# Two neighbouring rows to a partition, skipping by 256-row halves, a staggered loop and one DMA queue in a masked softmax after a matrix product

## The chip, the cores and the metric

The kernel runs on one core of one Trainium2 chip. The metric is the device time of one execution in microseconds (us). Each kernel was run several times, and the median of its fast runs is quoted.

## The reference, cut to what matters

```python
batch, m, k, n = 16, 512, 512, 512          # x: (16, 512, 512) float32, weight: (512, 512) float32
mask = (np.triu(np.ones((m, n))) == 0)      # true strictly below the diagonal

y = scale * np.matmul(x, weight)
y = np.where(mask == 1, y, -1e9)
y_exp = np.exp(y - np.max(y, axis=-1, keepdims=True))
out = (y_exp / np.sum(y_exp, axis=-1, keepdims=True)).astype(np.float32)
```

Row r of an output keeps only the columns below r, so about half of the products can be skipped. Row 0 keeps none and becomes the constant 1/512. Every execution must read 16.78 MB of x and write 16.78 MB of output.

## The kernel before

One batch passes through these steps. GpSimd (POOL) issues a load that converts float32 to bfloat16 on its way into one of 16 buffers. TensorE (PE) transposes x in sixteen 128x128 blocks, and VectorE (DVE) and ScalarE (ACT) copy one half each of the transposed x out of PSUM. PE makes the products. ACT takes the exponential and its row sums. DVE takes the reciprocal of the sums and scales the rows. SyncE (SP) issues the store.

```python
X_BUFS = 16
OUT_BUFS = 6
x_r = x.rearrange("b (mt p) k -> b p mt k", p=P)          # 2 KB runs: one row each
out_r = out.rearrange("b (mt p) n -> b p mt n", p=P)

def load(b):
    xb = x_pool.tile([P, MT, K], BF16, name="xb")
    nc.gpsimd.dma_start(xb, x_r[b])
# ... prepare(b): sixteen transposes, then one copy on DVE and one on ACT ...
def multiply(b):
    for mt in range(MT):
        NC = (mt + 1) * P                                  # 128, 256, 384, 512 columns
        # ... four matmuls of NC columns, one mask product, one exponential with row sums ...
def normalise(b):
    nc.vector.reciprocal(rinv, st_sum.pop(b))
    # ... four scalings on DVE ...
def store(b):
    nc.sync.dma_start(out_r[b], ots[b % OUT_BUFS])
# ...
for b in range(B):
    if b + 1 < B:
        prepare(b + 1)
    multiply(b)
    normalise(b)
    store(b)
    if b + X_BUFS < B:
        load(b + X_BUFS)
```

The softmax here doesn't subtract the row's maximum and nothing guards it: scores larger than these inputs give would overflow.

Of the kernel before, what the change touches and what calls it, by code (L numbers as in the profile page):

```python
# [1 line left out]

# [5 lines left out]

FP32 = mybir.dt.float32
BF16 = mybir.dt.bfloat16  # L10
AF = mybir.ActivationFunctionType
ALU = mybir.AluOpType

MASK_NEG = -512.0
P = 128
X_BUFS = 16
OUT_BUFS = 6


@with_exitstack  # L20
def kernel(
    ctx: ExitStack,
    tc: tile.TileContext,
    x: bass.AP,
    weight: bass.AP,
    scale: float,
    mask: bass.AP,
    out: bass.AP,
):






    nc = tc.nc

    B, M, K = x.shape
    K2, N = weight.shape
    assert K == K2 and N == 512 and K == 512 and M == 512  # L40
    MT = M // P
    KT = K // P

    const = ctx.enter_context(tc.tile_pool(name="const", bufs=1))
    x_pool = ctx.enter_context(tc.tile_pool(name="xf", bufs=X_BUFS))
    xt_pool = ctx.enter_context(tc.tile_pool(name="xt", bufs=2))
    sum_pool = ctx.enter_context(tc.tile_pool(name="sums", bufs=4))
    psum_t = ctx.enter_context(tc.tile_pool(name="psum_t", bufs=4, space=bass.MemoryType.PSUM))
    psum_y = ctx.enter_context(tc.tile_pool(name="psum_y", bufs=4, space=bass.MemoryType.PSUM))

    x_r = x.rearrange("b (mt p) k -> b p mt k", p=P)
    out_r = out.rearrange("b (mt p) n -> b p mt n", p=P)

    ident_bf = const.tile([P, P], BF16, name="ident_bf")
    w_f32 = const.tile([P, KT, N], FP32, name="w_f32")
    w_bf = const.tile([P, KT, N], BF16, name="w_bf")
    diag_f32 = const.tile([P, MT, P], FP32, name="diag_f32")
    diag_bf = const.tile([P, MT, P], BF16, name="diag_bf")
    ots = [const.tile([P, MT, N], FP32, name=f"ot{i}") for i in range(OUT_BUFS)]

    st_x, st_xt, st_py, st_sum = {}, {}, {}, {}

    def load(b):
        xb = x_pool.tile([P, MT, K], BF16, name="xb")
        nc.gpsimd.dma_start(xb, x_r[b])  # L65
        st_x[b] = xb

    def prepare(b):

        xb = st_x.pop(b)  # L70
        xt = xt_pool.tile([P, KT, M], BF16, name="xt")
        for h in range(2):
            pt = psum_t.tile([P, 2, M], BF16, name="pt")
            for kk in range(2):
                kt = 2 * h + kk
                for mt in range(MT):
                    nc.tensor.transpose(  # L77
                        pt[:, kk, mt * P : (mt + 1) * P],
                        xb[:, mt, kt * P : (kt + 1) * P],
                        ident_bf,  # L80
                    )
            if h == 0:
                nc.vector.tensor_copy(xt[:, 0:2], pt)  # L83
            else:
                nc.scalar.copy(xt[:, 2:4], pt)  # L85
        st_xt[b] = xt

    def multiply(b):
        xt = st_xt.pop(b)
        ot = ots[b % OUT_BUFS]  # L90
        rsum = sum_pool.tile([P, MT], FP32, name="rsum")
        for mt in range(MT):
            NC = (mt + 1) * P
            py = psum_y.tile([P, N], FP32, name="py")
            for kt in range(KT):
                nc.tensor.matmul(  # L96
                    py[:, :NC],
                    lhsT=xt[:, kt, mt * P : NC],
                    rhs=w_bf[:, kt, :NC],
                    start=(kt == 0),  # L100
                    stop=(kt == KT - 1),
                )
            nc.tensor.matmul(  # L103
                py[:, mt * P : NC],
                lhsT=ident_bf,
                rhs=diag_bf[:, mt],
                start=False,
                stop=True,
                skip_group_check=True,
            )  # L110
            nc.scalar.activation(  # L111
                out=ot[:, mt, :NC],
                in_=py[:, :NC],
                func=AF.Exp,
                bias=0.0,
                scale=float(scale),
                accum_out=rsum[:, mt : mt + 1],
            )
        st_sum[b] = rsum

    def normalise(b):
        ot = ots[b % OUT_BUFS]
        rinv = sum_pool.tile([P, MT], FP32, name="rinv")
        nc.vector.reciprocal(rinv, st_sum.pop(b))  # L124
        for mt in range(MT):
            NC = (mt + 1) * P
            nc.vector.tensor_scalar_mul(ot[:, mt, :NC], ot[:, mt, :NC], rinv[:, mt : mt + 1])  # L127
        nc.gpsimd.memset(ot[0:1, 0, :P], 1.0 / N)  # L128

    def store(b):  # L130
        nc.sync.dma_start(out_r[b], ots[b % OUT_BUFS])  # L131

    make_identity(nc, ident_bf)


    load(0)
    nc.sync.dma_start(w_f32, weight.rearrange("(kt p) n -> p kt n", p=P))
    for mt in range(MT):
        nc.sync.dma_start(diag_f32[:, mt], mask[mt * P : (mt + 1) * P, mt * P : (mt + 1) * P])
    for b in range(1, X_BUFS):  # L140
        load(b)

    for ot in ots:
        for mt in range(MT - 1):
            nc.gpsimd.memset(ot[:, mt, (mt + 1) * P :], 0.0)  # L145
        nc.gpsimd.memset(ot[0:1, 0, P:], 1.0 / N)  # L146

    prepare(0)
    for kt in range(KT):
        if kt % 2 == 0:  # L150
            nc.vector.tensor_copy(w_bf[:, kt], w_f32[:, kt])  # L151
        else:
            nc.scalar.copy(w_bf[:, kt], w_f32[:, kt])  # L153
    nc.vector.tensor_scalar(  # L154
        out=diag_bf,
        in0=diag_f32,
        scalar1=-MASK_NEG,
        scalar2=MASK_NEG,
        op0=ALU.mult,
        op1=ALU.add,  # L160
    )

    for b in range(B):
        if b + 1 < B:
            prepare(b + 1)
        multiply(b)
        normalise(b)
        store(b)
        if b + X_BUFS < B:
            load(b + X_BUFS)  # L170


# [1 line left out]
_INS = ['x', 'weight', 'scale', 'mask']  # L174
_OUTS = [((16, 512, 512), 'float32')]

_NUMBERS = {'scale': 0.125}


# [26 lines left out]
```

## Time and profile before

| | before |
|---|---|
| median time | 94.33 us (94.16 to 94.41, four runs) |
| span of the profiled execution | 92.4 us |
| busiest compute engine | PE, 62% of the span |
| DMA row of the slices | 9 (90% or more) in 37 of 40 slices |

The span is what the profiler sees of one execution. The device time stands some 2 us above it. The prediction shows the main lines of the page. Beside the engines named above, PEld stands for PE's loading of its stationary operand and SPq for the transfers that SP issues; "clock" (PEclk) is the share of PE's full clock that was granted.

DVE in the steady part, in the timeline (start, duration, engine, line, operation, tiles, and in brackets the idle time before it with its releaser):

```profile
64.89 0.69 DVE L83 COPY xt<-pt 128x1024 bf16<-128x1024 bf16 x1 [0.86 <-PE pt L77]
65.50 0.17 DVE L124 RECIPROCAL rinv<-rsum 128x4 f32<-128x4 f32 x1
65.76 1.29 DVE L127 TENSOR_SCALAR ot<-ot,rinv 128x128 f32<-128x128 f32 x4
```

### The profile page before, as it was taken

To read this page: it belongs to the slowest core of one execution; us is meant where nothing else is said; L and a number is where in the kernel's file an instruction comes from. 1 tells how busy PE (TensorE), PEld (TensorE's weight loads), DVE (VectorE), ACT (ScalarE), POOL (GpSimd) and SP (SyncE) were. 2 spreads that over 40 slices of the span, in tenths; PEclk is the share of its full clock that TensorE was granted. 3 is DMA by queue.
4 is the path that set the end of the run, shared out by engine and by line. 5 is a ranking of instruction groups with operands and counts; after the bars stand their busy time and mean duration, and the time that the engine had idled before them with its cause. 6 is when DMAs were issued, how large, how long until landed. Compare 5 with 4: busy or idle time off the path is not lost.

```text
span 92.4 us, 1586 instructions
## 1 busy us (share of the span) xinstructions
PE 57.5 (62%) x568; PEld 43.1 (47%) x576; DVE 37.2 (40%) x99; ACT 47.0 (51%) x147; POOL 25.3 (27%) x62
## 2 busy tenths in 40 slices
PE   0000599999999999900019774699999999600000
PEld 0000568867876876900016352576786786200000
DVE  0030212458546799300004217276845853650000
ACT  5040044998789873400034091899878878700000
POOL 5993333222333999800001001011101110110000
PEclk9999999999999999996555699999999999995555
DMA  1899999999999999999999999999999999999990
GB/s 27 335 220 191 208 206 206 206 206 207 206 206 207 208 208 206 206 206 283 290 286 291 285 337 403 397 407 403 408 406 407 401 407 407 409 408 410 408 353 33
DMA packets 18007, 26.57 MB, mean 288 GB/s; under 512 B 592, under 2 KB 9296, under 8 KB 18000
## 3 DMA queue, kind: packets, MB, share of 16 engines
q0 software_dynamic: 8448, 8.39, 54.7%
q1 hardware_dynamic: 9552, 18.09, 52.5%
q8 instruction: 4, 0.07, 0.3%
q14 instruction: 3, 0.02, 0.1%
HBM read 18.09 MB, written 16.78 MB: 377 GB/s over the span
## 4 chain that ended last, share of the span: by engine, by line
DMA 44%; PE 23%; POOL 17%; DVE 1%; issue 1%; ACT 1%; DVEq 0%; SPq 0%; ACTq 0%; POOLq 0%
DMA xb<-in_x_dram 24%; DMA out_dram<-ot 20%; PE py L96 17%; POOL xb L65 7%; POOL ot L145 7%; PE pt L77 5%; POOL ot L146 2%; PE py L103 2%; DVE ot L127 1%; ACT ot L111 1%; POOL ot L128 1%; POOL ident_bf masks.py:199 0%; DVEq L201 0%; SPq L131 0%; POOL ident_bf masks.py:197 0%
## 5 line engine op out<-in xcount | busy, mean ns | idle before, releaser
L96 PE MATMUL py<-w_bf,xt 128*128 128x128 bf16 (+3 forms) x248 | 42.6, 310 | 12.2 <-ACT ot L111 11.6
L111 ACT ACTIVATE ot<-py 128x128 f32<-128x128 f32 (+1 forms) x64 | 27.5, 443 | 18.2 <-DMA out_dram<-ot 14.9
L96 PEld LDWEIGHTS <-xt 128*128 128x128 bf16 x256 | 22.2, 102 | 21.5 <-issue 13.4
L77 PE MATMUL pt<-ident_bf,xb 128*128 128x128 bf16 x256 | 18.1, 230 | 10.2 <-DMA xb<-in_x_dram 10.2
L127 DVE TENSOR_SCALAR ot<-ot,rinv 128x128 f32<-128x128 f32 (+1 forms) x64 | 23.2, 445 | 1.6 <-DVE rinv L124 0.5
L85 ACT COPY xt<-pt 128x1024 bf16<-128x1024 bf16 x16 | 16.2, 1016 | 10.8 <-PE pt L77 8.5
L77 PEld LDWEIGHTS <-xb 128*128 128x128 bf16 x256 | 16.3, 104 | 11.6 <-DMA xb<-in_x_dram 10.2
L83 DVE COPY xt<-pt 128x1024 bf16<-128x1024 bf16 x16 | 11.0, 689 | 15.9 <-PE pt L77 14.2
L65 POOL DMA_DIRECT2D xb<-in_x_dram x16 | 12.2, 770 | 16.4 <-DMA xb<-in_x_dram 16.1
L128 POOL MEMSET ot<- 1x128 f32 x16 | 4.3, 287 | 39.4 <-DVE ot L127 39.4
L103 PE MATMUL py<-diag_bf,ident_bf 128*128 128x128 bf16 x64 | 14.4, 225 | 0.0
L111 ACT ACTIVATION_READ_ACCUMULATOR ot<-py 128x1 f32 x64 | 13.4, 210 | 0.0
L124 DVE RECIPROCAL rinv<-rsum 128x4 f32<-128x4 f32 x16 | 2.7, 172 | 18.1 <-ACT ot L111 18.1
L103 PEld LDWEIGHTS <-ident_bf 128*128 128x128 bf16 x64 | 6.5, 102 | 3.4 <-issue 0.5
L145 POOL MEMSET ot<- 128x384 f32 (+2 forms) x18 | 6.3, 383 | 0.0
L151 DVE CAST w_bf<-w_f 128x512 bf16<-128x512 f32 x2 | 0.9, 481 | 5.9 <-DMA w_f<-in_weight_dram 5.9
L153 ACT CAST w_bf<-w_f 128x512 bf16<-128x512 f32 x2 | 1.1, 616 | 3.9 <-DMA w_f<-in_weight_dram 3.9
L146 POOL MEMSET ot<- 1x384 f32 x6 | 2.4, 408 | 0.0
L154 DVE TENSOR_SCALAR diag_bf<-diag_f 128x512 bf16<-128x512 f32 x1 | 0.4, 427 | 3.6 <-DMA diag_f<-in_mask_dram 3.6
L153 ACT ACT_TABLE_LOAD x1 | 1.3, 1283 | 0.7 <-PEq L187 0.7
masks.py:199 POOL TENSOR_SCALAR_AFFINE_SELECT ident_bf<-ident_bf 128x128 bf16<-128x128 bf16 x1 | 0.3, 307 | 0.1
masks.py:197 POOL MEMSET ident_bf<- 128x128 bf16 x1 | 0.2, 206 | 0.3 <-POOLq L187 0.3
(4 smaller groups left out, 0.4 us busy)
## 6 DMA issues: line engine op xcount, KB each, us to landing
out_dram<-ot SPq DMA_DIRECT2D x16, 1024.0 KB, 11.6
xb<-in_x_dram POOLq DMA_DIRECT2D x16, 512.0 KB, 21.0
w_f<-in_weight_dram SPq DMA_DIRECT2D x1, 1024.0 KB, 5.1
diag_f<-in_mask_dram SPq DMA_DIRECT2D x4, 64.0 KB, 6.5
```

The costliest lines, as they stand in the source:

```text
L65: nc.gpsimd.dma_start(xb, x_r[b])
L77: nc.tensor.transpose(pt[:, kk, mt * P : (mt + 1) * P], xb[:, mt, kt * P : (kt + 1) * P], ident_bf,)
L83: nc.vector.tensor_copy(xt[:, 0:2], pt)
L85: nc.scalar.copy(xt[:, 2:4], pt)
L96: nc.tensor.matmul(py[:, :NC], lhsT=xt[:, kt, mt * P : NC], rhs=w_bf[:, kt, :NC], start=(kt == 0), stop=(kt == KT - 1),)
L103: nc.tensor.matmul(py[:, mt * P : NC], lhsT=ident_bf, rhs=diag_bf[:, mt], start=False, stop=True, skip_group_check=True,)
L111: nc.scalar.activation(out=ot[:, mt, :NC], in_=py[:, :NC], func=AF.Exp, bias=0.0, scale=float(scale), accum_out=rsum[:, mt : mt + 1],)
L124: nc.vector.reciprocal(rinv, st_sum.pop(b))
L127: nc.vector.tensor_scalar_mul(ot[:, mt, :NC], ot[:, mt, :NC], rinv[:, mt : mt + 1])
L128: nc.gpsimd.memset(ot[0:1, 0, :P], 1.0 / N)
L145: nc.gpsimd.memset(ot[:, mt, (mt + 1) * P :], 0.0)
L146: nc.gpsimd.memset(ot[0:1, 0, P:], 1.0 / N)
```

## The change

The intent: partition p holds rows 2p and 2p+1 of a 256-row half, so that each partition moves runs of 4 KB in place of 2 KB. All transfers go through SP's one hardware queue, so no POOL load stands before the fills of the output buffers. The loads now bring float32, so DVE converts. The loop is written staggered: the cast of batch i+2, the transposes of i+1, the products of i, then scaling and store of i-1. With pairs of rows in a partition, skipping goes by halves, with 256 and 512 columns in place of 128, 256, 384 and 512.

```diff
-X_BUFS = 16
+X_BUFS = 6
-    x_r = x.rearrange("b (mt p) k -> b p mt k", p=P)
-    out_r = out.rearrange("b (mt p) n -> b p mt n", p=P)
+    x_r = x.rearrange("b (h p s) k -> b p h (s k)", h=2, s=2)
+    out_r = out.rearrange("b (h p s) n -> b p h (s n)", h=2, s=2)
     def load(b):
-        xb = x_pool.tile([P, MT, K], BF16, name="xb")
-        nc.gpsimd.dma_start(xb, x_r[b])
+        xf = x_pool.tile([P, QT, K], FP32, name="xf")
+        nc.sync.dma_start(xf.rearrange("p (h s) k -> p h (s k)", h=2), x_r[b])
+    def cast(b):
+        xb = xb_pool.tile([P, QT, K], BF16, name="xb")
+        nc.vector.tensor_copy(xb, st_x.pop(b))
     ... multiply(b):
-            NC = (mt + 1) * P
+            h = q // 2
+            NC = (h + 1) * HB                 # HB = 256
     ... mask tiles, fills of the output buffers and start: cut ...
-    for b in range(B):
-        if b + 1 < B:
-            prepare(b + 1)
-        multiply(b)
-        normalise(b)
-        store(b)
-        if b + X_BUFS < B:
-            load(b + X_BUFS)
+    for i in range(B + 1):
+        if i + 2 < B:
+            cast(i + 2)
+        if i + 1 < B:
+            transpose(i + 1)
+        if i < B:
+            multiply(i)
+        if i >= 1:
+            normalise(i - 1)
+            store(i - 1)
+            if i - 1 + X_BUFS < B:
+                load(i - 1 + X_BUFS)
```

More of the change, by code (lines that the diff above doesn't have):

```diff
@@ L40 @@
     assert K == K2 and N == 512 and K == 512 and M == 512
-    MT = M // P
+    QT = M // P
     KT = K // P
+    HP = P // 2
+    HB = 2 * P
     const = ctx.enter_context(tc.tile_pool(name="const", bufs=1))
     x_pool = ctx.enter_context(tc.tile_pool(name="xf", bufs=X_BUFS))
-    xt_pool = ctx.enter_context(tc.tile_pool(name="xt", bufs=2))
+    xb_pool = ctx.enter_context(tc.tile_pool(name="xb", bufs=3))
+    xt_pool = ctx.enter_context(tc.tile_pool(name="xt", bufs=3))
     sum_pool = ctx.enter_context(tc.tile_pool(name="sums", bufs=4))
@@ L56, with transpose @@
     w_bf = const.tile([P, KT, N], BF16, name="w_bf")
-    diag_f32 = const.tile([P, MT, P], FP32, name="diag_f32")
-    diag_bf = const.tile([P, MT, P], BF16, name="diag_bf")
-    ots = [const.tile([P, MT, N], FP32, name=f"ot{i}") for i in range(OUT_BUFS)]
-    st_x, st_xt, st_py, st_sum = {}, {}, {}, {}
+    diag_f32 = const.tile([P, QT, P], FP32, name="diag_f32")
+    diag_bf = const.tile([P, QT, HB], BF16, name="diag_bf")
+    ots = [const.tile([P, QT, N], FP32, name=f"ot{i}") for i in range(OUT_BUFS)]
+    st_x, st_xb, st_xt, st_sum = {}, {}, {}, {}
     def load(b):
-        xb = x_pool.tile([P, MT, K], BF16, name="xb")
-        nc.gpsimd.dma_start(xb, x_r[b])
-        st_x[b] = xb
-    def prepare(b):
-        xb = st_x.pop(b)
-        xt = xt_pool.tile([P, KT, M], BF16, name="xt")
-        for h in range(2):
-            pt = psum_t.tile([P, 2, M], BF16, name="pt")
-            for kk in range(2):
-                kt = 2 * h + kk
-                for mt in range(MT):
-                    nc.tensor.transpose(
-                        pt[:, kk, mt * P : (mt + 1) * P],
-                        xb[:, mt, kt * P : (kt + 1) * P],
-                        ident_bf,
-                    )
-            if h == 0:
+        xf = x_pool.tile([P, QT, K], FP32, name="xf")
+        nc.sync.dma_start(xf.rearrange("p (h s) k -> p h (s k)", h=2), x_r[b])
+        st_x[b] = xf
+    def cast(b):
+        xb = xb_pool.tile([P, QT, K], BF16, name="xb")
+        nc.vector.tensor_copy(xb, st_x.pop(b))
+        st_xb[b] = xb
+    def transpose(b):
+        xb = st_xb.pop(b)
+        xt = xt_pool.tile([P, KT, QT, P], BF16, name="xt")
+        for half in range(2):
+            pt = psum_t.tile([P, 2, QT, P], BF16, name="pt")
+            for kk in range(2):
+                kt = 2 * half + kk
+                for q in range(QT):
+                    nc.tensor.transpose(pt[:, kk, q], xb[:, q, kt * P : (kt + 1) * P], ident_bf)
+            if half == 0:
                 nc.vector.tensor_copy(xt[:, 0:2], pt)
@@ L90, in multiply @@
         ot = ots[b % OUT_BUFS]
-        rsum = sum_pool.tile([P, MT], FP32, name="rsum")
-        for mt in range(MT):
-            NC = (mt + 1) * P
+        rsum = sum_pool.tile([P, QT], FP32, name="rsum")
+        for q in range(QT):
+            h = q // 2
+            NC = (h + 1) * HB
             py = psum_y.tile([P, N], FP32, name="py")
@@ L97, in multiply @@
                     py[:, :NC],
-                    lhsT=xt[:, kt, mt * P : NC],
+                    lhsT=xt[:, kt, q],
                     rhs=w_bf[:, kt, :NC],
@@ L103, in multiply @@
             nc.tensor.matmul(
-                py[:, mt * P : NC],
+                py[:, h * HB : NC],
                 lhsT=ident_bf,
-                rhs=diag_bf[:, mt],
+                rhs=diag_bf[:, q],
                 start=False,
@@ L111, in multiply @@
             nc.scalar.activation(
-                out=ot[:, mt, :NC],
+                out=ot[:, q, :NC],
                 in_=py[:, :NC],
@@ L116, in multiply @@
                 scale=float(scale),
-                accum_out=rsum[:, mt : mt + 1],
+                accum_out=rsum[:, q : q + 1],
             )
@@ L122, in normalise @@
         ot = ots[b % OUT_BUFS]
-        rinv = sum_pool.tile([P, MT], FP32, name="rinv")
+        rinv = sum_pool.tile([P, QT], FP32, name="rinv")
         nc.vector.reciprocal(rinv, st_sum.pop(b))
-        for mt in range(MT):
-            NC = (mt + 1) * P
-            nc.vector.tensor_scalar_mul(ot[:, mt, :NC], ot[:, mt, :NC], rinv[:, mt : mt + 1])
-        nc.gpsimd.memset(ot[0:1, 0, :P], 1.0 / N)
+        for q in range(QT):
+            NC = (q // 2 + 1) * HB
+            nc.vector.tensor_scalar_mul(ot[:, q, :NC], ot[:, q, :NC], rinv[:, q : q + 1])
+        nc.gpsimd.memset(ot[0:1, 0, :HB], 1.0 / N)
     def store(b):
-        nc.sync.dma_start(out_r[b], ots[b % OUT_BUFS])
-    make_identity(nc, ident_bf)
+        nc.sync.dma_start(out_r[b], ots[b % OUT_BUFS].rearrange("p (h s) n -> p h (s n)", h=2))
     load(0)
     nc.sync.dma_start(w_f32, weight.rearrange("(kt p) n -> p kt n", p=P))
-    for mt in range(MT):
-        nc.sync.dma_start(diag_f32[:, mt], mask[mt * P : (mt + 1) * P, mt * P : (mt + 1) * P])
+    for h in range(2):
+        for g in range(2):
+            r = h * HB + g * P
+            nc.sync.dma_start(
+                diag_f32[g * HP : (g + 1) * HP, 2 * h : 2 * h + 2],
+                mask[r : r + P, r : r + P].rearrange("(p s) c -> p s c", s=2),
+            )
     for b in range(1, X_BUFS):
         load(b)
+    make_identity(nc, ident_bf)
+    nc.gpsimd.memset(diag_bf[:HP, :, P:], MASK_NEG)
+    nc.gpsimd.memset(diag_bf[HP:, :, :P], 0.0)
     for ot in ots:
-        for mt in range(MT - 1):
-            nc.gpsimd.memset(ot[:, mt, (mt + 1) * P :], 0.0)
-        nc.gpsimd.memset(ot[0:1, 0, P:], 1.0 / N)
-    prepare(0)
+        nc.gpsimd.memset(ot[:, 0:2, HB:], 0.0)
+        nc.gpsimd.memset(ot[0:1, 0, HB:], 1.0 / N)
+    cast(0)
+    transpose(0)
     for kt in range(KT):
@@ L153 @@
             nc.scalar.copy(w_bf[:, kt], w_f32[:, kt])
-    nc.vector.tensor_scalar(
-        out=diag_bf,
-        in0=diag_f32,
-        scalar1=-MASK_NEG,
-        scalar2=MASK_NEG,
-        op0=ALU.mult,
-        op1=ALU.add,
-    )
-    for b in range(B):
-        if b + 1 < B:
-            prepare(b + 1)
-        multiply(b)
-        normalise(b)
-        store(b)
-        if b + X_BUFS < B:
-            load(b + X_BUFS)
+    for g in range(2):
+        nc.vector.tensor_scalar(
+            out=diag_bf[g * HP : (g + 1) * HP, :, g * P : (g + 1) * P],
+            in0=diag_f32[g * HP : (g + 1) * HP],
+            scalar1=-MASK_NEG,
+            scalar2=MASK_NEG,
+            op0=ALU.mult,
+            op1=ALU.add,
+        )
+    cast(1)
+    for i in range(B + 1):
[10 more added lines that the diff above has]
+                load(i - 1 + X_BUFS)
 _INS = ['x', 'weight', 'scale', 'mask']
```

## The prediction

> **What bounds the kernel now.** I read the page's slices first, because they say at once whether any resource is full from end to end.
>
> ```profile
> span 92.4 us, 1586 instructions
> PE 57.5 (62%) x568; PEld 43.1 (47%) x576; DVE 37.2 (40%) x99; ACT 47.0 (51%) x147; POOL 25.3 (27%) x62
> DMA  1899999999999999999999999999999999999990
> q0 software_dynamic: 8448, 8.39, 54.7%
> q1 hardware_dynamic: 9552, 18.09, 52.5%
> HBM read 18.09 MB, written 16.78 MB: 377 GB/s over the span
> ```
>
> No compute engine is above 62%, while the DMA row is full in 37 of 40 slices. One trap: the loads (q0) convert float32 to bfloat16 on the way and are counted by what they write, 8.39 MB, though they read 16.78 MB. So a load rate must be doubled to compare it with a store rate. I then cut the span into stretches (columns: stretch, length, busy PE, PEld, DVE, ACT, POOL, clock, DMA share, GB/s).
>
> ```profile
> 2.50:3.00 0.50, 0.00 (x0) 0.00 (x0) 0.00 (x0) 0.00 (x0) 0.50 (x2) 1.00 0.70 258
> 16.00:39.00 23.00, 22.79 (x263) 17.93 (x265) 15.47 (x37) 17.90 (x54) 12.89 (x36) 1.00 1.24 207
> 41.00:50.00 9.00, 1.83 (x12) 1.39 (x12) 0.34 (x2) 1.78 (x8) 0.00 (x0) 0.57 1.14 282
> 70.00:84.00 14.00, 9.86 (x97) 6.95 (x96) 7.42 (x23) 8.99 (x32) 1.37 (x4) 0.97 1.05 407
> 84.00:88.00 4.00, 0.00 (x0) 0.00 (x0) 0.00 (x0) 0.00 (x0) 0.00 (x0) 0.50 1.05 409
> 89.00:90.00 1.00, 0.00 (x0) 0.00 (x0) 0.00 (x0) 0.00 (x0) 0.00 (x0) 0.50 0.77 299
> ```
>
> Pure loading runs at 2 x 207 = 414 GB/s, pure storing at 407, the overlap of both at 282 as counted. The kernel is therefore bound by transfers in all three stages, and in 41 to 50 us the compute engines stand nearly still. The chain of waits shows the same, with a detail of the order:
>
> ```profile
> DMA 44%; PE 23%; POOL 17%; DVE 1%; issue 1%; ACT 1%; DVEq 0%; SPq 0%; ACTq 0%; POOLq 0%
> 7.09 21.73 DMA xb<-in_x_dram
> 29.85 0.82 POOL ot L145 x3
> 39.20 18.75 DMA out_dram<-ot
> ```
>
> The fills of the output buffers on POOL sit behind all the load issues, so the first store leaves only at 38 us. That delay looks expensive, but the transfer engines had loads to move meanwhile; it costs only what mixing costs later.
>
> **The budget of before.** In the windows, the first bytes amount to a full-rate start at about 2.5 us, and the thinning end to a full-rate end at about 89.95 us, which leaves 2.45 us to the end of the span. Between lie 87.4 us. Of these, x takes 16.78 MB / 0.414 = 40.5 us, the outputs 16.78 / 0.407 = 41.2 us, the weight 1.05 MB / 0.40 = 2.6 us, together 84.3 us. The mixed stretch: if 2 KB packets of loads (1 KB counted) and stores (2 KB) alternate, the pure rates would give about 308 GB/s counted; 285 over 13 us is 7% less, 0.9 us. The remaining 2.2 us are the mask's 512-byte runs and a start that is not quite full.
>
> **What the Trainium skill says.** (1) "DMA: Bandwidth & Descriptors", section Why small descriptors are slow: about 3 cycles of overhead per packet, with 32-byte beats. A 2 KB packet is then 67 cycles for 64 of data and a 4 KB one 131 for 128, a gain of 2.3%. The 407 here would become 416, my estimate from that page; the trace of before has no 4 KB packets to test it. (2) The same page, section iDMA fabric, gives 408.7 GB/s for one load stream from the SP queue in 1 MiB transfers with 4 KiB rows, the very form of the new loads. That is no better than this trace's 2 KB stores at 407, and speaks against (1). (3) The same page, Queues, rings and completion order: each engine takes turns between queues at packet boundaries, which fits the counted rate of the mixed stretch; the new kernel has one queue, so loads and stores run in issue order. (4) "VectorE: DVE Perf Modes", The perf-mode tier table: a float32 copy within SBUF runs at 2x, 1227 ns for 2048 elements. The trace agrees in kind: the 128x512 cast took 481 ns, and 1x would need over 533.
>
> **The change part by part.**
> Transfers: the same bytes (18.09 read, 16.78 written), in half as many packets, all through SP. The old loads' issue of 770 ns on POOL vanishes; it was hidden.
>
> PE: tiles of 128, 256, 384 and 512 columns become 256, 256, 512, 512, because two neighbouring rows share a partition and skipping goes by 256-row halves. From the chain, four matmuls take 0.22, 0.44, 0.65 and 0.86 us, a mask product of 128 columns 0.06, sixteen transposes 0.89. Before: 2.17 + 0.24 + 0.89 = 3.30 us per batch, which is the period seen at 61 to 75 us. After: 2 x 0.44 + 2 x 0.86 + 4 x 0.11 + 0.89 = 3.93 us. That is 0.63 us per batch, 10 us in all, more work.
>
> ACT: exponentials start 0.36 us apart at 256 columns and 0.57 at 512; four of the new ones take 1.86 us, with the 1.02 us copy 2.9 us.
>
> DVE: the new cast of 2048 elements, about 1.23 us; scalings 2 x 0.40 + 2 x 0.50 = 1.81 us; copy 0.69; reciprocal 0.17. At most 3.9 us.
>
> Against these stands one load plus one store, 2.10 MB, 5.1 us at 0.412. All three engines stay under it, so the added 10 us of PE lie beside transfers, if the queue never runs dry.
>
> **Can the one queue run dry?** SP is in order: load 0, weight, mask, loads 1 to 5, then store b and load b+6 in turn. The six loads, weight and mask keep the engines busy until about 2.5 + 7.34 MB / 0.412 + 1.5 = 21.8 us. Store 0 needs: load 0 landed near 6, cast, cold transposes (1.9 us for the first sixteen in the trace), weight converted near 10.5, products to 15, scaling to 17. So it leaves 4 us early. After that batches finish every 3.93 us and are wanted every 5.1, so slack grows. The fills of the output buffers now run at the start and no longer delay anything. At the end load 15 lands near 73.5; its cast, transposes, products and scaling take about 8 us, to 81.5; its store is wanted at 85, after stores 10 to 14. Six output buffers suffice: batch 15 needs the end of store 9 at about 71. Slack at the tightest places is 2 to 4 us.
>
> **The sum.** Start 2.5, weight 2.6, mask 1.5 (a guess inside the 2.2 us left over above), end 2.45; 33.55 MB of x and output at rate r. With r = 0.409: 82.0, span 91.05. With r = 0.416: 80.65, span 89.7. Timed runs stand 1.8 us above the span (94.16 against 92.4), so 92.8 and 91.5 us. I take r = 0.4125: 81.3, span 90.35, time 92.1 us. About 0.9 us of the 2.1 us gain come from the lost mixing, the rest from longer packets and a denser start.
>
> **Rivals.**
> (a) Longer runs buy nothing and only order helps: r about 0.408, 93 us, within 2%. For it: skill figure (2), and 2 KB loads here already at 414. Against: the loads at 414 write half as many bytes, so say little of float32 loads.
> (b) Directions in turn cost as packets in turn did: the mixed stretch was 7% slow. If the ten load-store pairs in the middle (21 MB) ran at 0.39 instead of 0.4125, that adds 2.9 us: 95 us, near or above before. Against: the new queue changes direction every megabyte, not every packet.
> (c) The queue runs dry: SP stops at a store's wait and the next load stands behind it. A late first store, or a PE at half clock, as in 41 to 50 us of the old trace (7.9 us per batch against 5.1), would cost 1 to 6 us. Against: the slack above, and waits of only about 1.2 us per batch.
> (d) Longer packets give the full 2.3% on loads and stores and the start is cleaner: r about 0.42, 90.8 us.
>
> **Range and chances.** The 2% line is 92.4 us, inside my two sums, so this is close: (d) and my centre fall on the faster side, (a) within, (b) and (c) split between within and slower. 92.1 us, range 90.3 to 94.4; faster 0.53, within 0.39, slower 0.08.
>
> **What would show it.** Right: DMA row full from slice 1 to the end, rate near 412 both in the middle and at the end, one hardware queue with about half the packets; PE busy about 63 us or more yet with short waits for loads late; first store by 18 us; last product 4 us or more before the last store ends. Wrong: a rate under 400 in the middle against 410 at the end (b), DMA slices below 9 in the middle or a clock near 0.5 (c), 418 or more (d). If the DVE cast takes over 2 us, DVE would reach 4.7 us and nearly be the bound.

## More of the kernel before

The program text is not the order in which an engine works. When the kernel is built, a scheduler sorts the instructions of each engine's queue, and the engine then takes them in that built order.

A row gives line, engine, operation, output and input, count, then busy us and mean ns of one, then the idle time of the engine just before such instructions and what ended most of it.

```profile
L111 ACT ACTIVATE ot<-py 128x128 f32<-128x128 f32 (+1 forms) x64 | 27.5, 443 | 18.2 <-DMA out_dram<-ot 14.9
L124 DVE RECIPROCAL rinv<-rsum 128x4 f32<-128x4 f32 x16 | 2.7, 172 | 18.1 <-ACT ot L111 18.1
```

The exponentials waited 14.9 us, in three waits, for stores to free output buffers. The longest, 9.1 us, ended at 47.75 us; it is the compute pause from 41 to 50 us that the prediction describes.

## The result

The changed kernel took **108.92 us** in the median (108.36 to 109.15, four runs) against 94.33 us, a ratio of 1.154 with a 95% interval of 1.149 to 1.159. It is slower by 15%, far outside the predicted range. A ratio here is the mean time of one kernel's fast runs over that of the other's in the same rounds, so it is not quite the ratio of the medians. Executions over 1.5% slower than the fastest of the same kernel are left out of the means.

First the page of the changed kernel. DMA and GB/s are 40 slices of the span, 2.67 us each, counted from 0 in what follows.

```profile
span 106.9 us, 1599 instructions
PE 73.2 (68%) x576; PEld 48.2 (45%) x576; DVE 57.0 (53%) x116; ACT 53.6 (50%) x147; POOL 14.9 (14%) x36
...
DMA  2998999999999999999999999999950724505354
GB/s 28 400 382 282 422 417 411 406 411 417 369 296 371 415 400 420 415 420 418 418 423 420 415 418 418 420 425 420 412 204 14 294 98 193 199 0 239 153 222 170
...
q1 hardware_dynamic: 9808, 34.87, 82.4%
```

There is one queue, with 9,808 packets where the two queues had 18,000, as intended. In slices 15 to 27 the rate is 415 to 425 GB/s, above the 414 of the old loads and the 407 of the old stores. Then, from slice 29 on (about 77.5 us), the DMA row falls to between 0 and 7. For the last 29 us the DMA engines have little to move. Yet no engine is over 68% busy. So something waits in a circle. The stretches show it too (columns as in the prediction: stretch, length, busy PE, PEld, DVE, ACT, POOL with counts, clock, DMA share, GB/s):

```profile
60.00:70.00 10.00, 6.14 (x59) 4.44 (x57) 6.87 (x14) 5.09 (x15) 0.90 (x2) 1.00 1.03 422
80.00:90.00 10.00, 6.14 (x54) 4.40 (x52) 6.89 (x14) 4.92 (x14) 0.90 (x2) 0.95 0.31 126
```

The engines work at the same pace in both, 61% on PE and 69% on DVE, whether the DMA engines are full (422 GB/s) or two thirds idle (126 GB/s). Computing does not wait for transfers here. It has a pace of its own, and that pace is below what the engines could do. The groups name the waits:

```profile
L104 PE MATMUL py<-w_bf,xt 128*128 128x256 bf16 (+1 forms) x256 | 56.6, 355 | 17.0 <-DVE xt L90 17.0
L132 DVE RECIPROCAL rinv<-rsum 128x4 f32<-128x4 f32 x16 | 2.8, 176 | 32.9 <-ACT ot L119 32.9
```

PE waits 17.0 us for DVE's copy of the transposed x, and DVE waits 32.9 us for ACT's exponentials. In the kernel before, DVE had waited 18.1 us there. Neither wait alone says why. The timeline of one period does:

```profile
62.51 0.83 PE L104 MATMUL py<-w_bf,xt 128*128 128x256 bf16 x6 [1.93 <-DVE xt L90]
...
65.45 0.27 PE L111 MATMUL py<-diag_bf,ident_bf 128*128 128x256 bf16 x1
...
65.76 0.60 ACT L119 ACTIVATE ot<-py 128x512 f32<-128x512 f32 x1 [0.28 <-PE py L111]
...
66.48 0.18 DVE L132 RECIPROCAL rinv<-rsum 128x4 f32<-128x4 f32 x1 [2.50 <-ACT ot L119]
...
66.75 1.14 DVE L135 TENSOR_SCALAR ot<-ot,rinv 128x256 f32<-128x256 f32 x3
...
67.82 0.67 DVE L90 COPY xt<-pt 128x1024 bf16<-128x1024 bf16 x1
68.41 0.47 DVE L135 TENSOR_SCALAR ot<-ot,rinv 128x512 f32<-128x512 f32 x1
...
68.55 0.83 PE L104 MATMUL py<-w_bf,xt 128*128 128x256 bf16 x6 [1.93 <-DVE xt L90]
```

Read it as a ring. PE makes the products of one batch from 62.51 to 65.7 us. ACT's last exponential and its sum end at 66.4. DVE then takes the reciprocal, then three of the four scalings of the same batch, and **only then** the copy of the next batch's transposed x, at 67.82. The next products cannot start before that, at 68.55. Period: 68.55 - 62.51 = 6.04 us. In the period before, which began at 54.80 us, it was 7.7 us; the clock granted to PE had sunk to 0.7 and 0.5 in slices 20 and 21 (53 to 59 us). No engine has 6 us of work in it (PE was busy for 4.1 us of this period, DVE for 3.5, ACT for 3.2), but the steps stand one behind the other.

The order in which the built program holds DVE's instructions (not a profile, and to be had without a chip) agrees with the timelines of both runs and shows that this is not chance. From batch 7 on, every batch of the changed kernel reads as on the left, and with the written order kept it reads as on the right:

```
changed kernel, as built                    with the order pinned (first experiment)
cast of a later batch                       cast of a later batch
reciprocal                                  copy of the transposed x
scaling, 256 columns, twice                 reciprocal
scaling, 512 columns                        scaling, 256 columns, twice
copy of the transposed x (next batch)       scaling, 512 columns, twice
scaling, 512 columns
```

On PE the transposes of batch j+1 stand behind the products of batch j. The written stagger is gone; the scheduler undid it.

What the ring costs can be read from SP's timeline, which shows when each store was issued:

```profile
49.17 0.38 SPq L139 DMA_DIRECT2D out_dram<-ot  x1
...
55.20 0.38 SPq L139 DMA_DIRECT2D out_dram<-ot  x1
...
62.91 0.38 SPq L139 DMA_DIRECT2D out_dram<-ot  x1
...
68.94 33.30 SPq L139 DMA_DIRECT2D out_dram<-ot  x6
```

Store 7 left at 49.17 us. The last row holds stores 10 to 15; the issue of store 15, 0.38 us long, ends at 68.94 + 33.30 and so began at 101.9 us. That is 52.7 us for eight batches, 6.59 us each, where their transfers take 5.1. Eight times 1.5 us is 12 us, most of the 14.5 us by which the span grew. It came to light late because the queue had a backlog. With load 13, issued right behind store 7 at 49.6 us, SP had issued loads 0 to 13, stores 0 to 7, the weight and the mask, 24.4 MB, of which some 18.3 MB had been moved by the slices. The 6.1 MB left, with the loads 14 and 15 and the stores 8 to 11, are 12.4 MB, which at 0.418 MB per us keep the DMA engines full until about 79 us. This is an estimate from issues and slices, and it fits slice 29 (77.5 to 80.2 us), the first since the start that is not full.

### The profile page after: what moved, and what is told of

Its sections match the earlier page's. It is cut to its first block, busy times and chain, and to the rows that moved or that the text cites. A ratio compares the mean times of both kernels' runs of the same rounds, so it can differ in the third digit from the quotient of the medians.

```text
span 106.9 us, 1599 instructions
## 1 busy us (share of the span) xinstructions
PE 73.2 (68%) x576; PEld 48.2 (45%) x576; DVE 57.0 (53%) x116; ACT 53.6 (50%) x147; POOL 14.9 (14%) x36
## 2 busy tenths in 40 slices
DMA packets 9814, 34.95 MB, mean 327 GB/s; under 512 B 592, under 2 KB 1104, under 8 KB 9808
## 3 DMA queue, kind: packets, MB, share of 16 engines
q1 hardware_dynamic: 9808, 34.87, 82.4%
## 5 line engine op out<-in xcount | busy, mean ns | idle before, releaser
L104 PE MATMUL py<-w_bf,xt 128*128 128x256 bf16 (+1 forms) x256 | 56.6, 355 | 17.0 <-DVE xt L90 17.0
L119 ACT ACTIVATE ot<-py 128x256 f32<-128x256 f32 (+1 forms) x64 | 31.2, 491 | 31.5 <-PE py L111 31.0
L104 PEld LDWEIGHTS <-xt 128*128 128x128 bf16 x256 | 25.9, 105 | 33.8 <-DVE xt L90 19.2
L135 DVE TENSOR_SCALAR ot<-ot,rinv 128x256 f32<-128x256 f32 (+1 forms) x64 | 25.2, 438 | 1.6 <-issue 0.5
L77 DVE CAST xb<-xf 128x2048 bf16<-128x2048 f32 x16 | 20.1, 1257 | 7.4 <-DMA xf<-in_x_dram 7.4
L132 DVE RECIPROCAL rinv<-rsum 128x4 f32<-128x4 f32 x16 | 2.8, 176 | 32.9 <-ACT ot L119 32.9
L136 POOL MEMSET ot<- 1x256 f32 x16 | 7.8, 484 | 85.6 <-DVE ot L135 85.6
L111 PE MATMUL py<-diag_bf,ident_bf 128*128 128x256 bf16 x64 | 18.8, 294 | 0.0
L159 POOL MEMSET ot<- 128x512 f32 x6 | 3.0, 520 | 0.1
L160 POOL MEMSET ot<- 1x256 f32 x6 | 2.7, 481 | 0.0
L170 DVE TENSOR_SCALAR diag_bf<-diag_f 64x512 bf16<-64x512 f32 x2 | 0.8, 416 | 0.0
L157 POOL MEMSET diag_bf<- 64x512 bf16 x1 | 0.5, 520 | 0.1
L156 POOL MEMSET diag_bf<- 64x512 bf16 x1 | 0.5, 523 | 0.0
```

The source lines that it names most:

```text
L77: nc.vector.tensor_copy(xb, st_x.pop(b))
L104: nc.tensor.matmul(py[:, :NC], lhsT=xt[:, kt, q], rhs=w_bf[:, kt, :NC], start=(kt == 0), stop=(kt == KT - 1),)
L111: nc.tensor.matmul(py[:, h * HB : NC], lhsT=ident_bf, rhs=diag_bf[:, q], start=False, stop=True, skip_group_check=True,)
L119: nc.scalar.activation(out=ot[:, q, :NC], in_=py[:, :NC], func=AF.Exp, bias=0.0, scale=float(scale), accum_out=rsum[:, q : q + 1],)
L135: nc.vector.tensor_scalar_mul(ot[:, q, :NC], ot[:, q, :NC], rinv[:, q : q + 1])
L136: nc.gpsimd.memset(ot[0:1, 0, :HB], 1.0 / N)
```

## The experiments

All ran with three rounds beside the kernel before, whose median was 94.16 to 94.32 us. All gave correct results except `e7_short_runs`.

| run | edit | us | ratio to before |
|---|---|---|---|
| e1_pinned | changed kernel, loop kept in written order | 95.99 | 1.017 |
| e2_one_pin | changed kernel, only the reciprocal kept in its place | 94.95 | 1.009 |
| e3_forced_late | late order forced from batch 0 | 121.12 | 1.286 |
| e4_copy_first | as e3, the copy ahead of the reciprocal | 100.34 | 1.067 |
| e5_ten_buffers | changed kernel, ten input buffers | 98.11 | 1.040 |
| e6_pinned_ten | written order and ten input buffers | **92.10** | **0.977** |
| e7_short_runs | e6 with 2 KB runs (wrong result) | 95.97 | 1.018 |
| e8_two_queues | e1 with loads issued by ACT | 100.26 | 1.064 |
| e9_pairs_alone | kernel before with the row pairs only | 92.17 | 0.978 |
| e10_cast_on_the_way | e1 with the old converting loads, 16 buffers | 92.89 | 0.985 |
| e11_one_pin_ten | e2 with ten input buffers | 97.48 (three fast runs) | 1.034 |
| e12_early_loads | e1 with each load issued earlier | **92.28** | **0.979** |

To pin an instruction means to mark it with `tc.keep_in_program_order`, so that the scheduler leaves it in its written place on its engine. The theory was that the built order closes the ring and costs most of the loss. The rivals were the wider products on PE, the cast on DVE, the one queue, and the two directions of transfer in turn.

### e1_pinned: the written order

```diff
+    pin = tc.keep_in_program_order
-        nc.vector.tensor_copy(xb, st_x.pop(b))
+        pin(nc.vector.tensor_copy(xb, st_x.pop(b)))
     ... likewise every other compute instruction of the loop on PE, DVE and ACT ...
```

> The changed kernel with every instruction of the batch loop held in program order on its engine (the same instructions, transfers and buffers). Theory (order): in the changed kernel the compiler's scheduler placed the copy of the next batch's transposed x on DVE behind three scalings of the current batch, so that products, exponentials, scaling and copy follow one another in a ring of 6.04 us per batch and the transfers run dry after 77 us. With the written order the copy stands before the scaling, the PE works at about 3.95 us per batch, transfers are full to the end: start 2.5 + weight 2.6 + mask 1.5 + 33.55 MB at 0.419 = 80.1 + end 2.45, span about 89, time 90 to 92 us. Rival (too few buffers or one queue: a load stands behind a store's wait): the order does not matter, the time stays at 105 or more with the same queue and the same six buffers.

Measured: 95.99 us (95.13 to 96.32). With the same arithmetic, the same widths, the same casts and the same queue, order alone is worth 12.9 us. The wider products, the cast and the one queue are all still there, so none of them can be the main cause. The size was not met, though: 90 to 92 us was expected. The slices show where the rest is:

```profile
GB/s 28 363 374 253 416 419 417 410 412 155 305 262 374 401 370 408 424 403 419 421 421 424 419 417 414 419 421 419 421 422 419 410 421 421 241 398 401 408 407 136
```

The late part is full now except for slice 34 (241). But from slice 9 to 12 (21 to 30 us) the rate falls to 155, 305, 262 and 374. SP issued store 0 at 23.11 us and only behind it load 6. The six buffers' loads had been moved by then, so the queue was dry. This is a second cause, and a smaller one; e6 and e12 deal with it. Store 0 is late through the written order itself: it left at 23.11 us here and at 18.24 us in the changed kernel. As written, the transposes of batch 1 stand ahead of the products of batch 0 on PE. They waited 4.68 us for DVE's cast, and the first products began at 15.60 us, against 10.15 in the changed kernel.

### e2_one_pin: one place in the order

```diff
-        nc.vector.reciprocal(rinv, st_sum.pop(b))
+        tc.keep_in_program_order(nc.vector.reciprocal(rinv, st_sum.pop(b)))
```

> The changed kernel with one instruction pinned: the reciprocal of each batch may not be placed ahead of what was written before it on DVE, which is the copy of the transposed x. The rest is left to the scheduler. Theory (order): that single edge breaks the ring, time 90 to 93 us. Rival (some other misplacement on PE or ACT matters as much): clearly slower than the fully pinned one, 95 us or more.

Measured: 94.95 us (94.54 to 95.67), 14.0 us less than the changed kernel, from one edit that adds no instruction. The expected 90 to 93 us were missed here too. But the rival asked for a time clearly above e1, and e2 even lies a little below it. The gap of e1 is there as well (207, 335, 275 and 338 GB/s in slices 9 to 12, store 0 at 22.53 us).

### e3_forced_late and e4_copy_first: closing the ring on purpose

```diff
 e3: in each step    products of i, transposes of i+1, reciprocal of i, three scalings of i,
                     copy of the transposed x of i+1, last scaling, store     (all pinned)
 e4: in each step    products of i, transposes of i+1, copy of the transposed x of i+1,
                     reciprocal of i, four scalings of i, store               (all pinned)
```

> All pinned as in e1, but in the order that the scheduler made for the later batches: products of a batch, transposes of the next, then on DVE reciprocal, three scalings, the copy, the last scaling. From the first batch on. Theory (order): the ring of about 6.04 us holds for all 16 batches: first product near 11 us, 16 x 6.04, then 2 us of scaling and 5 us of store: span near 112, time 108 to 117 us, and the store issues are 6 to 7.7 us apart. Rival (buffers, queue or DVE load made the changed kernel slow, the order is a symptom): near e1 or near the changed kernel's 109 with the same fast first half.

> As e3, with one thing moved: on DVE the copy stands before the reciprocal instead of behind the third scaling. The transposes still stand behind the products on PE. Theory (order): reciprocal and three scalings, about 1.4 us, leave the ring, but the second copy on ACT still waits for the last exponential; period 4.9 to 5.4 us, about the 5.0 us that transfers take per batch; time 93 to 104 us, at least 8 us under e3. Rival: the same as e3.

Measured: e3 took 121.12 us (120.90 to 121.44). Its first stores left at 19.34, 25.29 and 31.27 us and the last at 114.3, which makes 6.33 us per batch on the mean of fifteen. e4 took 100.34 us (100.14 to 101.01). Its first stores left at 18.02, 22.98 and 27.98 us and the last at 93.2, 5.01 us per batch from the start to the end. Two periods of the copy on DVE, first e3 and then e4:

```profile
36.11 0.67 DVE L96 COPY xt<-pt 128x1024 bf16<-128x1024 bf16 x1
...
42.09 0.67 DVE L96 COPY xt<-pt 128x1024 bf16<-128x1024 bf16 x1
```

```profile
30.61 0.69 DVE L96 COPY xt<-pt 128x1024 bf16<-128x1024 bf16 x1 [1.56 <-PE pt L90]
...
35.64 0.69 DVE L96 COPY xt<-pt 128x1024 bf16<-128x1024 bf16 x1 [1.56 <-PE pt L90]
```

At full clock a period is thus 5.97 us in e3 and 5.0 in e4. The clock row adds the rest: e4's PE had full speed in all slices but the last, while e3's sank to between 0.5 and 0.8 in seven of its last sixteen, where one period took 7.71 us. e3 lies above its expected range, which had reckoned with some 6.04 us in every period; the low clock made it 6.33 on the mean. The direction is what counts: with the same instructions, moving only the copy from behind three scalings to ahead of the reciprocal shortens every period and takes 20.8 us from the whole, some 5 us of it by e3's low clock. That the position of this one copy sets the pace is thereby shown. What remains of e4's loss is a shorter ring, in which the transposes still stand behind the products.

### e5_ten_buffers: more input buffers, order free

```diff
-X_BUFS = 6
+X_BUFS = 10
```

> The changed kernel with ten load buffers instead of six and nothing pinned. In the built program the scheduler, which now sees loads arrive early, places the copy of the next batch before the reciprocal in the later batches. Theory (order, made bad by the six buffers in the scheduler's own reckoning): no ring, PE near 4 us per batch, and the extra loads also fill the gap before the first stores: 90 to 92.5 us, faster than before by 2 to 4%. Rival (the order recovers but the gap of e1 and e2 at 21 to 28 us is something else than a lack of queued loads): 94 to 96 us as e1 and e2.

Measured: 98.11 us (97.42 to 98.42), a miss. The buffers did mend the first gap, and the built order did become another one, but not a good one. Now it is ACT whose copies for the next batches stand ahead of exponentials, and the queue runs dry from 74 to 83 us (309, 325, 10 and 132 GB/s in slices 31 to 34). So the built order depends on something as remote as the number of input buffers. How the scheduler reckons was only argued, and it stays open.

### e6_pinned_ten: both causes taken away

```diff
 e1, and
-X_BUFS = 6
+X_BUFS = 10
```

> e1 with ten load buffers. Theory: e1 lost about 3 us because loads 0 to 5 were all moved by about 21 us while store 0 was issued only at 23.1 us, and load 6 stands behind it in the one queue; four more loads are 10 us of transfers and cover that. Span about 90.5, time 91 to 92.5 us; DMA slices 9 to 13 near 415. Rival (the gap comes from the first batches' slow PE or from the stores themselves, and is only moved): 95 to 96 us as e1, with the gap at another place.

Measured: **92.10 us** (92.05 to 92.17), ratio 0.977 (0.9753 to 0.9787). It beats both kernels. Its timeline of DVE, beside the one of the changed kernel above:

```profile
63.37 0.69 DVE L92 COPY xt<-pt 128x1024 bf16<-128x1024 bf16 x1 [0.40 <-PE pt L90]
63.98 0.17 DVE L134 RECIPROCAL rinv<-rsum 128x4 f32<-128x4 f32 x1
64.24 1.53 DVE L137 TENSOR_SCALAR ot<-ot,rinv 128x256 f32<-128x256 f32 x4
...
67.30 0.69 DVE L92 COPY xt<-pt 128x1024 bf16<-128x1024 bf16 x1 [0.39 <-PE pt L90]
```

The copy waits for PE's transposes, not for ACT, and it comes first. The reciprocal behind it waits for nothing. The period is 67.30 - 63.37 = 3.93 us, PE's own work, exactly the figure of the prediction.

### e7_short_runs: what 4 KB runs are worth

```diff
 e6, and
-    x_r = x.rearrange("b (h p s) k -> b p h (s k)", h=2, s=2)
-    out_r = out.rearrange("b (h p s) n -> b p h (s n)", h=2, s=2)
+    x_r = x.rearrange("b (h s p) k -> b p h s k", h=2, s=2)
+    out_r = out.rearrange("b (h s p) n -> b p h s n", h=2, s=2)
```

The rows now lie where the mask tile does not expect them, so the result is wrong; sizes and work are those of e6.

> e6 with the rows of a half spread so that a partition's two rows are 128 rows apart: loads and stores move in runs of 2 KB instead of 4 KB; same bytes, instructions and order. The result is wrong on purpose (the mask no longer fits the rows). Theory (run length sets the rate): the rate falls from about 420 to the 407 of the old stores, 33.55 MB take 82.4 instead of 79.9 us: 2 to 3 us over e6. Rival (the higher rate of the changed kernel comes from the single queue or from float32 loads, not from the run length): within 0.7 us of e6.

Measured: 95.97 us (95.81 to 96.03), 3.9 us more than e6. The stretch from 24 to 36 us, where loads are most of what is moved, in e6 and then in e7, same columns as above:

```profile
24.00:36.00 12.00, 12.00 (x116) 8.77 (x114) 10.47 (x22) 9.59 (x29) 1.34 (x3) 1.00 1.03 413
```

```profile
24.00:36.00 12.00, 12.00 (x112) 8.64 (x110) 10.54 (x22) 9.44 (x28) 1.34 (x3) 1.00 1.05 390
```

PE is full in both, and only the rate differs: 413 against 390 GB/s. From 60 to 66 us it is 418 against 408. The longer runs are a real gain, larger than estimated.

### e8_two_queues: the loads in a queue of their own

```diff
 e1, and
-        nc.sync.dma_start(xf.rearrange("p (h s) k -> p h (s k)", h=2), x_r[b])
+        nc.scalar.dma_start(xf.rearrange("p (h s) k -> p h (s k)", h=2), x_r[b])
```

> e1 (six buffers, all pinned) with the loads issued from ACT, so that they no longer stand behind stores. Theory (the gap in e1 is loads standing behind store 0 in the one queue): loads 6 and 7 go as soon as their buffers are free, the gap at 21 to 28 us closes, 91.5 to 94 us; the ACT issues cost it 0.5 us per batch, beside other work. Rival (mixing directions between two queues costs as in the kernel before, where the mixed stretch ran 7% slow): the gap closes but the middle runs near 390 GB/s, 94 to 96 us.

Measured: 100.26 us (100.05 to 100.53), which neither theory expected. The first store left at 28.67 us, 5.6 us later than in e1. ACT now issues the loads, until 12.2 us, and began its first copy of a transposed x only then. But that is not what held the store back, as ACT's next copy waited for PE until 21.13 us. The timeline of DVE shows the reason:

```profile
15.67 0.42 DVE L172 TENSOR_SCALAR diag_bf<-diag_f 64x512 bf16<-64x512 f32 x1 [4.33 <-DMA diag_f<-in_mask_dram]
17.46 0.42 DVE L172 TENSOR_SCALAR diag_bf<-diag_f 64x512 bf16<-64x512 f32 x1 [1.37 <-DMA diag_f<-in_mask_dram]
17.92 1.23 DVE L79 CAST xb<-xf 128x2048 bf16<-128x2048 f32 x1
```

DVE converts the mask tile before it casts batch 1. In e1 the mask stood in SP's queue ahead of loads 1 to 5, its pieces took 6.6 us in the median from issue to landing, and DVE converted it at 10.04 us. In e8 the loads ran beside it from the other queue, its pieces took 12.4 us, and DVE waited for the last until 17.4. The cast of batch 1, its transposes on PE and the first products (20.88 us against 15.60) all came behind. As a test of one queue against two this run is inconclusive; e12 answers that. It has one use all the same. In its middle part (slices 20 to 30) loads and stores ran mixed from two queues at 416 to 424 GB/s. With one queue in turn e6 ran at 412 to 423 from 36 to 60 us. So neither way of mixing float32 loads with stores costs anything that can be seen here.

### e9_pairs_alone: the layout without the rest

```diff
 kernel before, and
-    x_r = x.rearrange("b (mt p) k -> b p mt k", p=P)
-    out_r = out.rearrange("b (mt p) n -> b p mt n", p=P)
+    x_r = x.rearrange("b (h p s) k -> b p h (s k)", h=2, s=2)
+    out_r = out.rearrange("b (h p s) n -> b p h (s n)", h=2, s=2)
     ... with the 256-row halves, mask tile and fills of the changed kernel ...
```

> The kernel before with only the layout of the change: two neighbouring rows to a partition, 4 KB runs in loads and stores, skipping by 256-row halves. Loads stay on the POOL queue with the conversion on the way, 16 buffers, and the output buffers are still filled behind all loads. The built order has the copy ahead of the reciprocal, so no ring. Theory: stores start near 37 us as before, the first output buffers come free near 54 us as before, and then ten batches must be computed at the new 3.95 us instead of 3.3: 54 + 39.5, then 2 us and the last store of 5: span about 98 to 101, time 99 to 103 us, compute-bound at the end. Rival (longer runs speed the transfers and that is all that counts): 90 to 92 us.

Measured: 92.17 us (91.88 to 92.47), ratio 0.978. The expectation missed. It assumed that the output buffers come free only at 54 us, so that the wider products would then be too late. The timeline of ACT shows when the exponentials resumed:

```profile
44.93 0.38 ACT L113 ACTIVATE ot<-py 128x256 f32<-128x256 f32 x1 [4.82 <-DMA out_dram<-ot]
```

They resumed at 44.93 us, and in the kernel before at 47.75. There was time enough for the wider products beside the stores. So the row pairs alone, with the halves they bring, on the old two queues and the old loop already give all that any version here reached. The one queue, the cast on DVE and the stagger bring nothing more.

### e10_cast_on_the_way: the old converting loads in the new loop

```diff
 e1, and
-        xf = x_pool.tile([P, QT, K], FP32, name="xf")
-        nc.sync.dma_start(xf.rearrange("p (h s) k -> p h (s k)", h=2), x_r[b])
+        xb = x_pool.tile([P, QT, K], BF16, name="xb")
+        pin(nc.gpsimd.dma_start(xb.rearrange("p (h s) k -> p h (s k)", h=2), x_r[b]))
     ... no cast on DVE, 16 buffers, the fills of the output buffers between the loads ...
```

> The pinned order of e6, but with the loads of the kernel before: from the POOL queue, converted to bfloat16 on the way, 16 buffers, in 4 KB runs, with the output buffers filled between the loads 5 and 12, so that stores start early. DVE has no cast. Theory (run length sets the rate, not queue or conversion): loads at 2 x 208 or more, no dry stretch, DVE 1.25 us per batch lighter: 91 to 93 us, within 1% of e6. Rival (packets from two queues taken in turn cost as in the mixed stretch of before, 7%): the middle falls to 390 GB/s as read, 94 to 96 us.

Measured: 92.89 us (92.74 to 93.00), 0.8 us above e6. Taking the 20 us of casts from DVE bought nothing, which speaks against the cast as a cost in the ordered versions. This run also changes the queue of the loads, so it does not single the cast out.

### e11_one_pin_ten: one pin, ten buffers

```diff
 e2, and
-X_BUFS = 6
+X_BUFS = 10
```

> Ten load buffers and the one pinned instruction of e2, the rest left to the scheduler. Theory (what e5 lost, it lost through the scheduler's order alone, and the pin on the reciprocal is enough where loads do not run out): 91 to 92.5 us, as e6. Rival (e5's copies on ACT stand ahead of the exponentials in the same way here, a second ring): 95 us or more, and transfers run dry after 70 us.

Measured: 97.48 us in the median of the three fast executions (97.07 to 98.19), and the ratio of 1.034 is theirs. A fourth, 99.24 us, was slow; with it the median is 97.83. It differs from e6 only in order, and the order is the ACT ring of e5:

```profile
58.31 1.01 ACT L92 COPY xt<-pt 128x1024 bf16<-128x1024 bf16 x1 [3.24 <-PE pt L88]
59.22 0.39 ACT L119 ACTIVATE ot<-py 128x256 f32<-128x256 f32 x1
...
59.75 0.60 PE L104 MATMUL py<-w_bf,xt 128*128 128x256 bf16 x4 [1.52 <-ACT ot L119]
```

ACT stood 3.24 us before a copy that needed PE's transposes, while the exponential behind it kept PE from its next products. The products of successive batches began at 53.81, 59.75, 66.84 and 72.24 us, some 6.1 us apart. One pin mends the ring that is there in the build with six buffers, and not the one in the build with ten. It is no recipe.

### e12_early_loads: six buffers, one queue, loads issued earlier

```diff
 e1, and
     def cast(b):
         ...
+        if b + X_BUFS < B:
+            load(b + X_BUFS)
     ... no load behind the store any more; loads and stores pinned too ...
```

> e1 (one queue, six load buffers, all pinned) with each further load written right behind the cast that frees its buffer, not behind a store: in the built program the one queue holds loads 0 to 9 ahead of store 0. Theory (e1's gap is a load that stands behind a store's wait in the one queue; neither the number of buffers nor the single queue costs anything by itself): no dry stretch, 91.5 to 92.7 us as e6. Rival (it was the four more buffers): 95 to 96 us as e1, with a gap near 21 to 28 us.

Measured: **92.28 us** (92.04 to 92.51), ratio 0.979, 3.7 us below e1. Its slices:

```profile
GB/s 15 346 371 295 387 420 422 409 409 407 407 407 409 407 420 417 424 417 409 418 418 426 411 417 417 420 420 422 418 422 406 426 415 426 417 418 424 420 326 35
```

No slice from 4 to 37 is under 387. Store 0 left at 23.61 us, no earlier than e1's 23.11, but now loads 0 to 9 stood ahead of it. So the gap of e1 came neither from too few buffers nor from there being one queue. It came from a load standing behind a store's wait, when its buffer had long been free.

## Why the prediction was wrong

**The step that failed** is the sentence "All three engines stay under it, so the added 10 us of PE lie beside transfers, if the queue never runs dry", with its follower "After that batches finish every 3.93 us and are wanted every 5.1, so slack grows". It took the sum of each engine's work as the pace of the batch. That is so only if the engines' instructions stand in an order that lets them overlap. In the built order a batch took 6.04 us at full clock, and 6.59 us on the mean of the last eight. The written order with ten input buffers (e6) gave the predicted 3.93. The order of the built program can be had without a chip, before any run; the prediction does not speak of it.

**A second step failed**, and was hidden behind the first: under "Can the one queue run dry?", store 0 was to be ready at 17 us, so that "it leaves 4 us early". The prediction had computed the kernel as written, but as written, with its six buffers and each load behind a store (e1), it takes 95.99 us and not 92.1. Its store 0 left at 23.11 us, and the queue was dry in part from 21 to 30 us. The predicted time comes out only with ten buffers (92.10 us in e6) or with loads issued earlier (92.28 us in e12).

**The work of the engines** was sized rightly. PE's busy time rose from 57.5 to 65.6 us in e6 and 67.2 in e1, 8 to 10 us against 10 predicted (73.2 in the changed kernel itself, part of which ran at a granted clock of 0.5 to 0.7). A cast on DVE took 1,257 ns against the 1.23 us expected, in line with the table of perf modes that the prediction cites. In the changed kernel the first store left at 18.24 us against about 17.

**The rate** was too low in the sum: 0.4125 was taken, and slices 15 to 27 ran at 0.415 to 0.425. Rival (d), at 0.42, was right about it, and rival (a), in which longer runs buy nothing, falls with e7. That the total of 92.1 agrees with e6 to the digit is partly luck: the higher rate is offset by a start that was less dense than assumed (slices of 338, 379 and 275 GB/s in e6).

**Rival (b)**, that directions in turn cost something, is refuted: e6 ran its mixed part at 412 to 423 GB/s, and e8 at 416 to 424.

**Rival (c)**, that the queue runs dry, is the right family. Its causes, a late first store and a half clock, were the smaller part. The first appears in e1 as 3.7 us, by comparison with e12; in the changed kernel the store was in time and the gap slight (369, 296 and 371 GB/s in slices 10 to 12). The half clock stretched a period from 6.04 to 7.7 us. But "1 to 6 us" stands against 16.8 us between the changed kernel and e6, because a ring through four steps and three engines was not on the list.

**What stays open**: why the scheduler chose that order. e5 shows that it changes with the number of buffers, and no run shows by what reckoning. How PE's half clock arises was not tested either.

## What to carry to other kernels

When a changed loop is slow and no engine is full, find one period in the timeline and follow it around: a wait of PE for DVE, of DVE for ACT and of ACT for PE is a ring, and its length, not any engine's sum, is the pace. Before predicting the gain of a stagger, read the order of the built program on each engine and ask of each instruction whose result the ones ahead of it need; a copy that feeds the next batch belonged here ahead of what finishes this one (5.0 us per batch in e4 against 5.97 in e3). In a queue that serves both directions, put each load where its buffer comes free, not behind a store that must wait.

## What the Trainium skill lacked or had wrong

- "TensorE: Matmul & The Clock Gate", section Architectural detail, states that the queues of ACT and DVE are strict FIFO. The runs agree: a copy ready to go stood behind three scalings in every late batch. The page doesn't say what follows from it, that an order fixed at build time can close a ring over engines that are each far from full. Here that was 6.04 us per batch where no engine was busy for more than 4.1 us, and 108.92 us against 94.95 us with one instruction kept in its place.
- "DMA: Bandwidth & Descriptors", section Why small descriptors are slow, led to an estimate of 2.3% for going from 2 KB to 4 KB. The estimate took only the first of the two costs that the section names; with the second, 32 bytes of metadata for each operation, it would be about 3.0%, an estimate from that section too. The runs show 3.9 us of 92.1 us, 4.2%: 390 against 413 GB/s where loads dominate, 408 against 418 later.
- The same page, section Issuing engines are not separate DMA queues, says that issuing from several engines saves only the time of issue. It leaves out what the place of issue decides. A load standing behind a store's wait cost 3.7 us (95.99 us in e1, 92.28 us in e12), and loads in a second queue beside the mask held the mask back until 17.4 us and the first store until 28.67 (100.26 us in e8).
